# Fifteen input tiles made ahead, weight sums on another engine, a projection on six banks, an affine step in place, and a new order of products in one kernel

## The chip, the cores and the metric

One core of a Trainium2 chip runs the whole program as one launch. The time is device time in microseconds of that core, the median of three runs. Its engines are TensorE (PE, with PEld for loading weights into it), VectorE (DVE), ScalarE (ACT), GpSimd (POOL) and SyncE (SP), which issues nearly all DMAs. SBUF holds the tiles that the engines work on, and the eight PSUM banks hold what PE accumulates.

## What is computed

One decoder layer for a prompt of 2048 tokens and eight samples of 8 tokens each, 2112 token columns in all, model width 1024, everything in float32:

```python
mod = silu(c) @ w_ada + b_ada                      # six modulation vectors: sh1, sc1, g1, sh2, sc2, g2
h = rmsnorm(x, norm_mix_w) * (1 + sc1) + sh1
qkv, z, b, a, sq, sk, sv = split(h @ w_in)         # input projection
o_dn = deltanet(causal_conv4(qkv), z, b, a)        # gated DeltaNet, 4 heads, chunks
o_swa = attend(sq, sk, sv)                         # window of 128, 8 heads, sinks, relative bias
x = x + g1 * (concat(o_dn, o_swa) @ w_out)
h = rmsnorm(x, norm_ffn_w) * (1 + sc2) + sh2
gate, up = split(causal_conv3(h @ ffn_w_up) + ffn_conv_b)
x = x + g2 * ((silu(gate) * up) @ ffn_w_down)      # width 2816 in between
y = rmsnorm(x, final_norm_w)
```

The outputs are y for all tokens, the last inputs of both convolutions, the DeltaNet states and the window's keys and values.

## The kernel before

**Tiling.** Activations lie transposed, 128 channels on the partitions and tokens in columns. The tokens come in two halves: half 0 has two blocks of 512 columns, half 1 blocks of 384, 384 and 320 columns, the last with the samples' 64 (`HALVES`, line 37). A weight tile is 128 x 1024 (`load_split`, L325). Each float32 operand is split into a high part, a rounded copy made by ACT (L330), and a low part, the difference, made by DVE or POOL (L331); a product is then three matmuls, hi x hi, hi x lo and lo x hi (`gemm_steps`, L339).

**Order.** Work is written as generators that are interleaved: `beside(steps, filler, share)` runs a filler's steps between those of other work, `lockstep` takes one step of each of several in turn, `chain` one after the other. Every engine executes its own instructions in one fixed order, which a planner of the framework lays out when the program is built. An engine that waits therefore holds up all that stands behind it. A pool's tile with a tag and a number of buffers is a ring: a new tile of that tag waits until the oldest one has been read for the last time.

**Stages** (times from the trace, in us): until about 66 the modulation vectors and the first products of the input projection; to 237 `inproj(0, ...)` for rows 2 to 11, beside `tasks` (the rest of the modulation, `weight_sums` for units 0 to 5, the gates, and `x_rstd` for half 1); to 350 `inproj(0, ...)` for rows 12 to 21, beside `ahead(0)`, the DeltaNet's first two chunks; to about 730 `mixers(0)` (DeltaNet scan and attention) beside `inproj(1, ...)`, whose rest runs to 797; then `between(0)` with the output projection, `ffn_in` (residual, norm, h of the second branch) and the FFN's up projection; then the same for half 1; from 1657 to 2177 the second part of the up projection; from 2177 on `down_phase`.

**What the change touches.**

- `affine_h` (L235) makes h from x: a DMA loads x into a tile `ht` of the tag "cv" (L261 to L263), DVE multiplies it by scale and norm (L264), then either ACT adds the shift into `hi` (L270) and DVE makes `lo` (L271), or, for every second k, ACT adds the shift in place (L266), ACT casts (L267) and POOL makes `lo`. Where the source is a list of tiles already in SBUF (the first block of the kernel, and the last block of `ffn_in`), `ht` is still taken from "cv" and the list's tile is read. The samples' part (`hst`, L251) uses a "cv" tile as well.
- The ring "cv" has five buffers (`CV = 5`). It also holds `ev`, the output of a projection's convolution (`conv_block`: `rb`, a raw copy, at L537, `ev` or `cv` at L540 or L542, three taps on DVE at L547) and the other results of `in_evac` (L600 to L608).
- `second` makes all of half 1's h, 24 tiles and the samples' one, when half 0's projection gives up its last two h tiles, one block after the other.
- `inproj(1, ...)` accumulates in the two PSUM banks "acc"; `FREE_TAGS` names six banks, which `between` uses for its own projections.
- `weight_sums` (L1621) combines two rows of the down projection's weights in four DVE instructions of 128 x 512 (L1632 to L1635), through one buffer "suv", and stores them to `ws_d`; six of 11 units run beside the first input projection, the others later.
- `down_phase` (L1648) multiplies in seven products of half-size blocks instead of eight (a Strassen scheme), over two passes of tokens; each product has 11 k tiles and takes four output blocks by 11 x 3 matmuls. `DOWN` (L1643) gives the products' order, their weight operand (A or S), their token operand (B or T), and the outputs to which each adds. `get_t` loads the token operand and combines it where needed: T2 = B22 - T1, T4 = T1 + E. T1, T3 and E come from `ts_d`, which the up projection stores. All raw loads go to rings of `RAWS = 4`; "tr" and "wr" lie in the pool `ds`, "tx" and "x" in the pool `dr`, opened when the up projection's pools are closed. `norm` is the last RMSNorm with its stores, run as steps between later products.

Of the kernel before, what the change touches and what calls it, by code (L numbers as in the profile page):

```python
# [94 lines left out]
def kernel(  # L95
# [138 lines left out]

    def affine_h(hb, bi, hf, branch, rB, src, ks=range(KT), pool_too=lambda k: k % 2, smp=None):  # L235
# [21 lines left out]
        for k in ks:  # L257
            h, l = hi[:, k, :np_], lo[:, k, :np_]
            t = x = gw.tile([P, 512], F32, tag="cv", name="ht", bufs=CV)[:, :np_]
            if isinstance(src, list):  # L260
                x = src[k][:, :np_]  # L261
            else:
                nc.sync.dma_start(x, src[k, :, c0:c0 + np_])  # L263
# [354 lines left out]

    def inproj(hf, h, ic, ms, **kw):
        return project(ms, "in_ps", lambda m: load_split(I["w_inT"][m], nc.gpsimd if hf and m % 2 else nc.vector), h, hf,  # L620
                       lambda m, bi, ps: in_evac(hf, bi, m, ps, ic), **kw)
# [999 lines left out]
    def weight_sums(units, pool):  # L1621

        tt = nc.vector.tensor_tensor
        cut = lambda t: (t[:, :D // 2], t[:, D // 2:])
        for i in units:
# [17 lines left out]
    DOWN = [("A11", "B11", 1, True, [(0, 1)]), ("S2", "T2", 1, False, [(0, 2)]), ("S3", "T3", 2, False, [(1, 1), (1, 2)]),  # L1643
            ("S1", "T1", 2, True, [(1, 2)]), ("S4", "B22", 2, False, [(0, 2)]), ("A22", "T4", 1, True, [(1, 1)]),
            ("A12", "B21", 1, True, [(0, 1)])]
    NM = KT // 2

    def down_phase(ds, dr, pd):  # L1648
# [28 lines left out]
        def load(tag, src, n, most, bufs):  # L1677

            raw = (dr if tag == "tx" else ds).tile([P, most], F32, tag=tag, name=tag, bufs=bufs)[:, :n]
# [10 lines left out]
        w, t = {}, {}  # L1690
# [7 lines left out]
        def get_t(q, i, r):  # L1698
# [4 lines left out]
            get = lambda tag, name, r, bufs: load(tag, t_src(q, name, i, r), r.stop - r.start, big, bufs)  # L1703
            if name == "T2":
                raw, more = get("tr", "T1", r, RAWS), get("tx", "B22", slice(r.start, min(r.stop, PW)), RAWS)
                c = more.shape[1]
                nc.vector.tensor_tensor(raw[:, :c], more, raw[:, :c], ALU.subtract)
                if c < raw.shape[1]:
                    nc.scalar.mul(raw[:, c:], raw[:, c:], -1.0)
            elif name == "T4":  # L1710
                raw, more = get("tr", "T1", r, RAWS), get("tx", "E", r, RAWS)
                nc.vector.tensor_tensor(raw, raw, more, ALU.add)
            else:
                raw = get("tr", name, r, RAWS)
            t[q, i, r.start] = halves(ds, "t", raw, big, DR)

        def blocks_of(q, g=None):

            if q < ND or q % ND in (3, 4):
# [456 lines left out]
```

## Time and profile before

| | |
|---|---|
| runs shown | 2650.94 us median of 3 (2646.79 to 2656.68) |
| the profiled execution | 2652.56 us, of which the span of its instructions is 2650.8 us |
| mean granted TensorE clock | 0.990 |
| DMA | 445.31 MB in 325327 packets, mean 168 GB/s |

The profile shows one execution. Its span runs from the first to the last instruction; the execution's own time lies 1.8 us above it. The page gives the busy time of each engine, the chain of work that ended last, the costliest groups of instructions, and, with the trace, who made an engine wait, the single instructions in time, and for any stretch the busy time of each engine with the granted clock. TensorE's matmuls on 512 columns start 227 ns apart where nothing disturbs them, those on 384 columns 174 ns apart. In rows of one instruction the columns are start in us, duration in us, engine, line, operation, out <- in with shapes, and in brackets the idle time of the engine before it with what ended it; rows of a group have the count, then minimum, median and maximum in ns and the stretch in which they ran; rows of waits have the total, the count and the longest, in us.

### The profile page before, as it was taken

The numbers are of one execution on the slowest core, as the hardware profiler recorded it, in microseconds if no ns is written. First come the engines' busy times: TensorE is split into PE (matmuls) and PEld (weight loads), VectorE is DVE, ScalarE is ACT, GpSimd is POOL, SyncE is SP. The second block draws the span as 40 slices with busy tenths as digits, with TensorE's granted clock in tenths as the row PEclk, the third lists the DMA queues.
The fourth block names the chain that finished last, engine by engine and source line by source line (L and its number), as shares of the span: only waits on it lengthen the run. The fifth ranks groups of instructions, "written<-read, shape, count | busy, mean of one in ns | idle before, by whom it ended". The sixth has DMA issues, their size and how long they took to land.

```text
span 2650.8 us, 45631 instructions
## 1 busy us (share of the span) xinstructions
PE 2564.9 (97%) x16424; PEld 2223.7 (84%) x16424; DVE 1838.0 (69%) x3657; ACT 1284.4 (48%) x3124; POOL 757.6 (29%) x677
## 2 busy tenths in 40 slices
PE   7999989999999899999999999999999999999998
PEld 5677878888897787777777789999999997889988
DVE  7475469887443677888868664886777666676676
ACT  5453355564342455455444353554555554554343
POOL 2031133233332412223211123335555520020012
PEclk9999989999999999999999999999999999999999
DMA  7787454334456253343226357424555459678673
GB/s 288 247 301 236 134 151 118 101 97 115 106 176 205 103 144 98 105 108 102 76 92 215 130 181 225 144 67 156 171 170 186 166 183 302 214 237 279 214 250 130
DMA packets 325327, 445.31 MB, mean 168 GB/s; under 512 B 83267, under 2 KB 207268, under 8 KB 324836
## 3 DMA queue, kind: packets, MB, share of 16 engines
q1 hardware_dynamic: 325100, 442.39, 52.7%
q8 instruction: 129, 2.11, 0.3%
q14 instruction: 98, 0.80, 0.1%
HBM read 322.74 MB, written 120.57 MB: 167 GB/s over the span
## 4 chain that ended last, share of the span: by engine, by line
PE 70%; DVE 12%; DMA 9%; ACT 3%; issue 3%; SPq 2%; POOL 1%; DVEq 0%; POOLq 0%; ACTq 0%
PE up_ps L339 15%; PE dn_ps L1795 15%; PE in_ps L339 12%; PE uq_b L1585 5%; PE op_ps L339 4%; PE uq_c L1585 2%; PE uq_u L1585 2%; PE uq_g L1585 2%; DVE ev L547 2%; PE pv_ps L1007 1%; PE uq_a L1585 1%; DMA mt<-mixd 1%; PE as_ps L970 1%; DVE w_lo L331 1%; DMA suv<-in_w_downT_dram 1%
## 5 line engine op out<-in xcount | busy, mean ns | idle before, releaser
L339 PE MATMUL in_ps<-hi,w_hi 128*128 128x512 f32 (+2 forms) x880 | 320.4, 367 | 10.0 <-ACT ev L608 5.6
L339 PE MATMUL up_ps<-hi,w_hi 128*128 128x512 f32 (+2 forms) x808 | 315.0, 390 | 7.3 <-ACT cv L542 7.3
L339 PE MATMUL in_ps<-lo,w_hi 128*128 128x512 f32 (+2 forms) x880 | 316.6, 360 | 2.4 <-DVE lo L271 2.0
L339 PE MATMUL in_ps<-hi,w_lo 128*128 128x512 f32 (+2 forms) x880 | 314.9, 358 | 0.0
L339 PE MATMUL up_ps<-lo,w_hi 128*128 128x512 f32 (+2 forms) x808 | 313.9, 388 | 0.0
L339 PE MATMUL up_ps<-hi,w_lo 128*128 128x512 f32 (+2 forms) x808 | 311.8, 387 | 0.0
L1795 PE MATMUL dn_ps<-th,wh 128*128 128x512 f32 (+2 forms) x796 | 272.2, 343 | 4.5 <-DVE x L1263 4.2
L1795 PE MATMUL dn_ps<-tl,wh 128*128 128x512 f32 (+2 forms) x796 | 272.2, 342 | 3.6 <-DVE tl L1687 3.6
L1795 PE MATMUL dn_ps<-th,wl 128*128 128x512 f32 (+2 forms) x796 | 270.8, 342 | 0.0
L331 DVE TENSOR_TENSOR w_lo<-w_raw,w_hi 128x1024 fp32r<-128x1024 f32 x115 | 145.7, 1267 | 82.8 <-ACT w_hi L330 81.3
L330 ACT CAST w_hi<-w_raw 128x1024 fp32r<-128x1024 f32 x126 | 132.0, 1047 | 145.9 <-PE op_ps L339 52.2
L339 PEld LDWEIGHTS in_ps<-hi,w_hi 128*128 128x128 f32 x880 | 166.6, 190 | 36.7 <-issue 7.8
L339 PEld LDWEIGHTS in_ps<-lo,w_hi 128*128 128x128 f32 x880 | 167.1, 190 | 26.2 <-issue 7.6
L339 PEld LDWEIGHTS up_ps<-hi,w_hi 128*128 128x128 f32 x808 | 152.6, 189 | 41.9 <-issue 8.6
L339 PEld LDWEIGHTS up_ps<-lo,w_hi 128*128 128x128 f32 x808 | 152.7, 189 | 35.1 <-issue 10.7
L339 PEld LDWEIGHTS in_ps<-hi,w_lo 128*128 128x128 f32 x880 | 166.8, 190 | 15.6 <-issue 1.6
L339 PEld LDWEIGHTS up_ps<-hi,w_lo 128*128 128x128 f32 x808 | 152.4, 189 | 31.4 <-issue 5.3
L1795 PEld LDWEIGHTS dn_ps<-th,wh 128*128 128x128 f32 x796 | 150.7, 190 | 21.9 <-DVE x L1263 3.9
L1795 PEld LDWEIGHTS dn_ps<-tl,wh 128*128 128x128 f32 x796 | 150.9, 190 | 19.1 <-DVE tl L1687 3.9
L1795 PEld LDWEIGHTS dn_ps<-th,wl 128*128 128x128 f32 x796 | 150.8, 189 | 15.6
L1686 ACT CAST wh<-wr 128x512 fp32r<-128x512 f32 x149 | 92.1, 618 | 143.7 <-PE dn_ps L1795 115.5
L547 DVE SCALAR_TENSOR_TENSOR ev<-rb,cw,ev 128x512 f32<-128x512 f32 (+2 forms) x180 | 132.3, 739 | 31.4 <-ACT ev L540 29.6
(547 smaller groups left out, 6493.5 us busy)
## 6 DMA issues: line engine op xcount, KB each, us to landing
w_raw<-in_w_upT_dram SPq DMA_DIRECT2D x50, 512.0 KB
wada<-in_w_ada_dram SPq DMA_DIRECT2D x48, 512.0 KB
w_raw<-in_w_inT_dram SPq DMA_DIRECT2D x44, 512.0 KB
wr<-ws_d SPq DMA_DIRECT2D x88, 256.0 KB
w_raw<-in_w_outT_dram SPq DMA_DIRECT2D x34, 512.0 KB
d<-act_d SPq DMA_DIRECT2D x33, 512.0 KB
wr<-in_w_downT_dram SPq DMA_DIRECT2D x66, 256.0 KB
tr<-T_d SPq DMA_DIRECT2D x66, 256.0 KB
```

The source lines that it names most:

```text
L330: nc.scalar.copy(hi, raw)
L331: (eng or nc.vector).tensor_tensor(lo, raw, hi.bitcast(F32), ALU.subtract)
L339: nc.tensor.matmul(ps[:, :n], a[:, k, :], b[:, k, :n], start=first is not False and k == ks[0] and i == 0, stop=last is not False and k == ...
L547: nc.vector.scalar_tensor_tensor(out, src(j), w[:, j:j + 1], out, ALU.mult, ALU.add)
L970: nc.tensor.matmul(banks[v][:, 256 * g:256 * g + 256 - P * k0], qs[:, 2 * (g0 + g) + v], t[:, v, :2 - k0].rearrange("p w j -> p (w j)"), s ...
L1007: nc.tensor.matmul(pv_ps[64 * v:64 * v + 64, :], (vprev[0], vt)[half][:, 64 * v:64 * v + 64], PT[v, half], start=half == k0, stop=half == 1)
L1585: nc.tensor.matmul(bk[t][:, :nb], u[:, k], v[:, k], start=new and k == 0 and y == 0, stop=k == KG - 1 and y == 2, skip_group_check=True)
L1686: nc.scalar.copy(h, raw)
L1795: nc.tensor.matmul(acc[m, s][:, :n], w[q, i][a][:, c], th[b][:, v], start=new and i == 0 and y == 0, stop=i == KH - 1 and y == 2, skip_gro ...
```

## The change

It has five parts.

**A.** The first six units of `weight_sums` run on POOL (`nc.gpsimd`) instead of DVE; the later five stay on DVE.

**B.** A new generator `early_h` makes 15 of half 1's 24 h tiles (block 0, k 0 to 7, and block 1, k 0 to 6) in lockstep with `ahead(0)`: it loads x, lets DVE multiply and ACT add the shift, all in place, in buffers that belong to the mixers' pool and are not yet in use there (tags "xz", "qs", "kh", "kl", "u", "o", "nl", "pt" and "PT"). `affine_h` then finds such a tile in `made` and only copies it to `hi` (ACT) and makes `lo`.

**C.** `inproj` takes its PSUM tags from a list `in_tags`, ["acc"] at first; after `mixers(0)` it is set to `FREE_TAGS`, six banks in turn, for what is left of `inproj(1, ...)`.

**D.** Where `affine_h`'s source is a list, the affine is made in place in the list's tile, without a "cv" tile.

**E.** `down_phase` begins with the products of T1 and B22, whose operands stay in SBUF (`held`: 11 tiles each for T1 and B22, one buffer per tile); T2 and T4 are then made from the held tiles with no second load. "tr" moves to the pool `dr`; "wr" and T1's first four tiles lie in `ds`. The tiles x have one buffer instead of two. `FINAL` names, for each output, the product that completes it, and the norms start accordingly.

```diff
+    made = {}
+    def early_h(pool):
+        def spare(tag, bufs=1, size=1):
+            t = pool.tile([P, 4 * size, P], F32, tag=tag, name="he", bufs=bufs).rearrange("p h i -> p (h i)")
+            return [t[:, 512 * i:512 * i + 512] for i in range(size)]
+        room = iter(spare("xz") + spare("qs", 1, 2) + spare("kh") + spare("kl") + spare("u") + spare("o")
+                    + spare("nl", 3) + spare("nl", 3) + spare("nl", 3) + spare("pt") + [spare("PT", 4)[0] for _ in range(4)])
+        for i, t in enumerate(room):
+            bi, k = divmod(i, KT)
+            c0, n = HALVES[1][bi]
+            t = made[bi, k] = t[:, :n]
+            nc.sync.dma_start(t, I["xT"][k, :, c0:c0 + n])
+            nc.vector.scalar_tensor_tensor(t, t, MOD[:, 1, k, 0:1], rB_tile(1, bi), ALU.mult, ALU.mult)
+            nc.scalar.activation(t, t, AF.Identity, bias=MOD[:, 0, k, 0:1], scale=1.0)
+            yield True
...
-            t = x = gw.tile([P, 512], F32, tag="cv", name="ht", bufs=CV)[:, :np_]
+            if (bi, k) in made:
+                t = made.pop((bi, k))
+                nc.scalar.copy(h, t)
+                (nc.gpsimd if pool_too(k) else nc.vector).tensor_tensor(l, t, h.bitcast(F32), ALU.subtract)
+                yield True
+                continue
             if isinstance(src, list):
-                x = src[k][:, :np_]
+                t = x = src[k][:, :np_]
             else:
+                t = x = gw.tile([P, 512], F32, tag="cv", name="ht", bufs=CV)[:, :np_]
...
+    in_tags = ["acc"]
     def inproj(hf, h, ic, ms, **kw):
         return project(ms, "in_ps", lambda m: load_split(I["w_inT"][m], nc.gpsimd if hf and m % 2 else nc.vector), h, hf,
-                       lambda m, bi, ps: in_evac(hf, bi, m, ps, ic), **kw)
+                       lambda m, bi, ps: in_evac(hf, bi, m, ps, ic), **{"tags": in_tags, **kw})
...
-    def weight_sums(units, pool):
-        tt = nc.vector.tensor_tensor
+    def weight_sums(units, pool, eng):
+        tt = eng.tensor_tensor
...
-    DOWN = [("A11", "B11", 1, True, [(0, 1)]), ("S2", "T2", 1, False, [(0, 2)]), ("S3", "T3", 2, False, [(1, 1), (1, 2)]),
-            ("S1", "T1", 2, True, [(1, 2)]), ("S4", "B22", 2, False, [(0, 2)]), ("A22", "T4", 1, True, [(1, 1)]),
-            ("A12", "B21", 1, True, [(0, 1)])]
+    DOWN = [("S1", "T1", 2, True, [(1, 2)]), ("S4", "B22", 2, False, [(0, 2)]),
+            ("A11", "B11", 1, True, [(0, 1)]), ("S2", "T2", 1, False, [(0, 2)]), ("S3", "T3", 2, False, [(1, 1), (1, 2)]),
+            ("A22", "T4", 1, True, [(1, 1)]), ("A12", "B21", 1, True, [(0, 1)])]
+    FINAL = {(0, 2): 3, (1, 2): 4, (1, 1): 5, (0, 1): 6}
...
-            raw = (dr if tag == "tx" else ds).tile([P, most], F32, tag=tag, name=tag, bufs=bufs)[:, :n]
+            raw = (ds if tag in IN_DS else dr).tile([P, most], F32, tag=tag, name=tag, bufs=bufs)[:, :n]
...
+        w, t, held = {}, {}, {}
+        IN_DS = ["wr"] + [f"cT1_{i}" for i in range(RAWS)]
...
-            get = lambda tag, name, r, bufs: load(tag, t_src(q, name, i, r), r.stop - r.start, big, bufs)
-            if name == "T2":
-                raw, more = get("tr", "T1", r, RAWS), get("tx", "B22", slice(r.start, min(r.stop, PW)), RAWS)
-                c = more.shape[1]
-                nc.vector.tensor_tensor(raw[:, :c], more, raw[:, :c], ALU.subtract)
-                if c < raw.shape[1]:
-                    nc.scalar.mul(raw[:, c:], raw[:, c:], -1.0)
-            elif name == "T4":
-                raw, more = get("tr", "T1", r, RAWS), get("tx", "E", r, RAWS)
-                nc.vector.tensor_tensor(raw, raw, more, ALU.add)
+            n = r.stop - r.start
+            if name in ("T1", "B22"):
+                m = wide(q, 1) if name == "T1" else PW
+                held[name, i] = load(f"c{name}_{i}", t_src(q, name, i, slice(0, m)), m, big if name == "T1" else PW, 1)
+                raw = held[name, i][:, r]
+            elif name == "T2":
+                raw = dr.tile([P, big], F32, tag="tr", name="tr", bufs=RAWS)[:, :n]
+                nc.vector.tensor_tensor(raw[:, :PW], held["B22", i], held["T1", i][:, :PW], ALU.subtract)
+                if n > PW:
+                    nc.scalar.mul(raw[:, PW:], held["T1", i][:, PW:], -1.0)
             else:
-                raw = get("tr", name, r, RAWS)
+                raw = load("tr", t_src(q, "E" if name == "T4" else name, i, r), n, big, RAWS)
+                if name == "T4":
+                    nc.vector.tensor_tensor(raw, raw, held["T1", i][:, r], ALU.add)
             t[q, i, r.start] = halves(ds, "t", raw, big, DR)
...
-            if q < ND or q % ND in (3, 4):
+            if q < ND or q % ND in (0, 1):
...
-                    if j < 3:
+                    if j < FINAL[og, tg]:
...
-                x[o] = dr.tile([P, NM, big], F32, tag=f"x{o[0]}{o[1]}", name=f"x{o[0]}{o[1]}", bufs=2)
+                x[o] = dr.tile([P, NM, big], F32, tag=f"x{o[0]}{o[1]}", name=f"x{o[0]}{o[1]}", bufs=1)
...
-                finish = norm(*late, free[-2:], wait=2 - ip)
-            elif j == 6:
-                late = (1, 0, PW, x, sums[1], cols[1])
-            elif j == 2 and ip:
-                finish = norm(*late, free[-2:], wait=2)
+                rest(finish or ())
+                finish = norm(*late, free[-2:])
+            elif j == 6 and not ip:
+                finish = chain(finish, norm(1, 0, PW, x, sums[1], cols[1], free[-2:], wait=2))
...
-                  spaced(weight_sums(range(6), sa), 2)),
+                  spaced(weight_sums(range(6), sa, nc.gpsimd), 2)),
...
-            beside(ahead(0, mp), filler, SHARE[0])
+            beside(lockstep(ahead(0, mp), early_h(mp)), filler, SHARE[0])
...
+        in_tags[:] = FREE_TAGS
...
-            beside(lockstep(sample_delta(sp), sample_attend(sp), weight_sums(range(6, KH), sp)), filler, SHARE[2])
+            beside(lockstep(sample_delta(sp), sample_attend(sp), weight_sums(range(6, KH), sp, nc.vector)), filler, SHARE[2])
```

More of the change, by code (lines that the diff above doesn't have):

```diff
@@ L1688, in halves @@
             return h, l
-        w, t = {}, {}
+        w, t, held = {}, {}, {}
+        IN_DS = ["wr"] + [f"cT1_{i}" for i in range(RAWS)]
         def get_w(q, i):
```

## The prediction

> **What bounds the kernel now.** I read the page's span and busy times first, then who made TensorE wait, then the granted clock in short stretches.
>
> ```profile
> span 2650.8 us, 45631 instructions
> ...
> PE 2564.9 (97%) x16424; PEld 2223.7 (84%) x16424; DVE 1838.0 (69%) x3657; ACT 1284.4 (48%) x3124; POOL 757.6 (29%) x677
> ```
>
> PE is busy for 97% of the span. The change removes no matmul, so it can only win back time in which PE stands still or runs slowly. Who made it wait:
>
> ```profile
> PE up_ps L339 <- ACT cv L542: 7.3, 1, 7.3
> PE z_ps L785 <- DVE T L806: 7.2, 2, 6.4
> PE in_ps L339 <- ACT ev L608: 5.6, 2, 3.6
> ...
> PE op_ps L339 <- ACT ev L608: 2.4, 1, 2.4
> ```
>
> A few single waits stand out, all between stages. I took a stretch around each, and the stretches of low clock that go with them (columns: window, length, busy PE, PEld, DVE, ACT, POOL, granted clock, DMA share, GB/s):
>
> ```profile
> 230.00:244.00 14.00, 10.78 (x39) 8.42 (x38) 8.72 (x15) 2.64 (x5) 5.89 (x9) 0.76 0.70 228
> 350.00:392.00 42.00, 30.36 (x272) 27.17 (x271) 35.71 (x84) 30.09 (x92) 19.69 (x16) 0.80 0.53 143
> 786.00:804.00 18.00, 13.56 (x71) 11.69 (x70) 7.30 (x8) 8.35 (x15) 6.49 (x5) 0.91 0.62 187
> 908.00:926.00 18.00, 10.66 (x43) 8.40 (x42) 14.98 (x18) 10.16 (x18) 9.16 (x9) 0.81 0.04 15
> 2186.00:2216.00 30.00, 24.75 (x100) 19.41 (x99) 17.59 (x28) 11.95 (x22) 0.00 (x0) 0.94 0.90 313
> ...
> 235.90:243.00 7.10, 5.99 (x14) 4.74 (x15) 3.74 (x8) 1.77 (x3) 5.68 (x9) 0.52 0.74 240
> 355.40:362.30 6.90, 5.38 (x18) 5.38 (x18) 4.58 (x11) 5.68 (x18) 3.64 (x2) 0.51 0.62 197
> 375.90:386.10 10.20, 6.00 (x52) 4.51 (x52) 9.89 (x26) 5.17 (x13) 2.88 (x4) 0.51 0.21 57
> ...
> 799.20:802.70 3.50, 3.27 (x7) 2.24 (x8) 2.81 (x3) 1.85 (x4) 0.25 (x1) 0.51 0.38 117
> 915.20:922.10 6.90, 3.70 (x9) 2.93 (x10) 5.99 (x7) 4.05 (x8) 5.49 (x7) 0.51 0.00 0
> 2205.40:2208.90 3.50, 3.50 (x10) 2.69 (x10) 2.37 (x4) 0.62 (x1) 0.00 (x0) 0.52 1.06 397
> ```
>
> Length less PE busy is idle; of the time busy at half clock, half is lost. So the five places cost: **A** (230) 3.2 + 3.0 = 6.2 us; **B** (350) 11.6 + 2.7 + 3.0 = 17.3; **C** (786) 4.4 + 1.6 = 6.0; **D** (908) 7.3 + 1.9 = 9.2; **E** (2186) 5.3 + 1.8 = 7.1. The sum, 45.8 us or 1.7%, is about all that these edits can reach. Each meets one of them.
>
> **A: weight sums on POOL.** 24 adds and subtracts (six units of four) leave DVE's queue.
>
> ```profile
> 228.97 0.69 DVE L1632 TENSOR_TENSOR suv<-suv 128x512 f32<-128x512 f32 x1 [1.90 <-DMA suv<-in_w_downT_dram]
> ...
> 232.77 2.32 DVE L547 SCALAR_TENSOR_TENSOR ev<-rb,cw,ev 128x512 f32<-128x512 f32 x3
> 236.27 0.69 DVE L603 SCALAR_TENSOR_TENSOR ev<-ev,in_ps 128x512 f32<-128x512 f32 x1 [1.18 <-ACT ev L602]
> ...
> L1275 POOL TENSOR_TENSOR dsum<-dsum,sq 128x512 f32<-128x512 f32 x14 | 19.4, 1386 | 190.5 <-ACT sq L1274 190.5
> ```
>
> The convolution taps (L547) stand behind a unit: 1.9 us of waiting for its load and 4 x 0.69 = 2.8 us of work. ACT's silu and L603 (236.27) wait for the taps, and PE, idle for 3.2 us of this window, for L603. Without the unit the taps move up by nearly 4.7 us, more than the 3.2 us stall. POOL, busy for 5.9 of the window's 14 us, pays 4 x 1.39 = 5.6 us a unit (the 128x512 add of L1275), 2.8 us more; the units follow one another through one buffer, so the last ends up to 14 us later. Queued behind it on POOL are the first chunk's masks, which are not needed while input projections fill PE. If that cover fails, I allow 3 us of loss. **Value 5, between -3 and 6.2.**
>
> Against it speaks that POOL and DVE slow one another:
>
> ```profile
> L1632 DVE TENSOR_TENSOR suv<-suv x11: 677/692/1502, 139.4 to 1474.2; 128x512 f32<-128x512 f32 x11
> ...
> L284 POOL TENSOR_TENSOR xacc<-xacc,xst x21: 863/1210/1609, 128.6 to 188.7; 128x384 f32<-128x384 f32 x14, 128x320 f32<-128x320 f32 x7
> ```
>
> The DVE add takes 0.69 us, and up to 1.50 us in the stretch in which POOL adds. If each of POOL's four adds holds the taps up by the difference, 0.81 us, that gives back 3.2 us of the 4.7. What remains, 1.5 us, is less than the stall; A is then worth about 1.5, a rival below. [...]
>
> **B: fifteen tiles made early.** Where the projection changes to the second token half, 24 tiles of h (and the samples' one) are made at once:
>
> ```profile
> L264 DVE SCALAR_TENSOR_TENSOR ht<-ht,MOD,sg x24: 462/608/1346, 343.9 to 391.6; 128x384 f32<-128x384 f32 x16, 128x256 f32<-128x256 f32 x8
> ...
> L266 ACT ACTIVATE ht<-ht,MOD x12: 508/613/625, 346.8 to 392.3; 128x384 f32<-128x384 f32 x8, 128x256 f32<-128x256 f32 x4
> L267 ACT CAST hi<-ht x12: 392/502/523, 348.2 to 393.2; 128x384 fp32r<-128x384 f32 x8, 128x256 fp32r<-128x256 f32 x4
> ...
> 365.86 0.47 ACT L537 COPY rb<-in_ps 128x384 f32<-128x384 f32 x1
> ...
> 386.64 0.58 ACT L540 ACTIVATE ev<-in_ps,cw 128x384 f32<-128x384 f32 x1
> ...
> 376.03 1.67 DVE L251 TENSOR_TENSOR hst<-hst,MOD 128x512 f32<-128x512 f32 x1 [2.90 <-DMA hst<-in_xT_dram]
> ...
> 265.00:331.00 66.00, 66.00 (x420) 52.97 (x419) 31.50 (x99) 21.59 (x46) 7.85 (x11) 1.00 0.45 133
> ```
>
> Of one and the same product, ACT copies rb at 365.86 and writes ev only at 386.64: ev needs one of five "cv" buffers, and 25 tiles stand ahead in them. Fifteen leave this ring. At this place DVE is spared 15 x 0.608 = 9.1 us and ACT 15 x 0.613 - 8 x 0.502 = 5.2 us (seven of the 15 pay the affine and a cast now, eight the affine alone; made early, each pays one copy here, at the cast's price), besides 15 loads. The same work, with 15 loads more on SP, is put beside the stretch 265 to 331, where DVE is busy 31.5 of 66 us and PE all of it; there it costs nothing. If a load is late there, DVE waits, but PE has two accumulators of 5.4 us each as cover. What is left are ten tiles on five buffers, the wait for hst among them, so I don't take the whole 17.3. The early tiles sit in the attention's buffers; its loads wait until they are copied out. The first two thirds of the stall (3.6 us, and the 20 us of ev) should go, a wait for the last token block stay. **Value 11, between 3 and 17** (below nothing only by the rival S).
>
> **C: six accumulators.** Both waits at 786 are for a free accumulator. But the output projection needs its weights:
>
> ```profile
> 797.48 0.62 ACT L1182 CAST mixh<-mt 128x512 fp32r<-128x512 f32 x1 [2.23 <-DMA mt<-mixd]
> 798.01 1.04 ACT L330 CAST w_hi<-w_raw 128x1024 fp32r<-128x1024 f32 x1
> ```
>
> w_hi is there at 799.05 and PE goes on at 799.4. If ACT keeps its order, PE only waits longer once instead of twice, and 0.4 us is won; if the cast comes ahead of the late mixh, all 6.0. **Value 2.5.**
>
> **D: affine in place.** The same ring of five, in the next change of stage:
>
> ```profile
> 904.60 0.59 ACT L537 COPY rb<-up_ps 128x512 f32<-128x512 f32 x1 [1.89 <-PE up_ps L339]
> ...
> 917.59 0.76 ACT L542 ACTIVATE cv<-up_ps,fcb,fcw 128x512 f32<-128x512 f32 x1
> ...
> 908.76 3.38 DVE L264 SCALAR_TENSOR_TENSOR ht<-x,MOD,rb_ps 128x512 f32<-128x512 f32 x5 [4.49 <-PE rb_ps L222]
> ```
>
> The write of cv waits 13 us for a buffer, with eight tiles of h ahead. In place they take none, and cv is written at about 905.3, while DVE is idle (4.49 us). Then PE waits for h itself: eight tiles from 908.8 on, at 1.5 DVE operations of 0.74 us each, so up to 917.6, used by PE as they come; it ends about 4 us earlier than now, and part of the low clock goes. **Value 5, between 1 and 9.** At the start of the kernel the same edit is taken at nothing; the steps there are paced by the adaLN loads.
>
> **E: the down projection.** T1 and B22 are kept, 11 tiles each, which saves 33 loads a pass, 66 in all. After the start that is worth nothing: PE is busy throughout there.
>
> ```profile
> 2253.00:2319.00 66.00, 66.00 (x293) 54.68 (x292) 40.09 (x62) 32.92 (x60) 4.19 (x3) 1.00 0.66 213
> ...
> 2201.93 0.69 DVE L1707 TENSOR_TENSOR tr<-tx,tr 128x512 f32<-128x512 f32 x1 [7.88 <-DMA wr<-ws_d]
> ...
> 2189.30 0.32 SPq L1496 DMA_DIRECT2D E_d<-d  x1
> 2189.71 0.41 SPq L1827 DMA_DIRECT2D x<-x2T  x1
> 2190.18 2.26 SPq L1680 DMA_DIRECT2D tx<-act_d  x3
> ```
>
> At the start, DVE waits for the loads of L1707 with the tile that PE needs behind it; the new order has no such combination there. But only four T1 tiles lie in the pool "ds"; the rest lie in "dr", and the first loads into dr (x, tx) were issued only behind the last store of the up projection, at 2189.3. PE enters this stage at 2177 and has 4 x 12 matmuls x 0.225 (66.00 us for 293 in the window above) = 10.8 us of work with four tiles, up to 2187.8. Issued at 2189.7, landed in 3 us and split in 1.3, the fifth comes at about 2194: 6.2 us idle with some half clock, about today's loss. If dr is free at 2177, all 7.1 goes. If the load takes as long as the first tx (2190.2 to 2201.9), PE idles 15 + 1.8 and E loses 10. **Value 1, between -10 and 7.** The norms and the single x buffers lie beside products of 30 us each: nothing.
>
> **The sum.** 5 + 11 + 2.5 + 5 + 1 = 24.5 us off the execution's 2652.6 (span 2650.8): **2628 us**. The median shown, 2650.9, is 0.06% below that execution; I let the two stand for one.
>
> **Rivals.**
> - The late ten tiles keep the ring full: B gives 3, in all 16.5: 2636. For it, hst's load alone stopped DVE for 2.9 us.
> - POOL holds DVE up: A gives 1.5: 2632.
> - T1 is late by the full landing time: E is -10, in all 13.5: 2639. The issue at 2189.7 speaks for it, the short list of loads ahead against it.
> - All five stalls vanish: 2607. Against it stand C's weights and D's h.
> - **S, slower:** the attention's qs, kh, kl and nl buffers, held by early tiles, come free only about 356 to 360, and PE's fixed order keeps the attention's scores ahead of the products, as at 351.7 now. PE idles some 10 us more, with 3.4 us of half clock, beside today's stall; no B, with A, C, D and E at their weak ends (-3, 0.4, 1, -3): 2652.6 + 13.4 + 4.6 = 2671. It decides from the point where the first qs cast comes after about 360.
>
> **How the numbers follow.** Forecast 0.45, ring 0.17, POOL 0.08, late T1 0.13, all gone 0.08, S 0.09. The range 2608 to 2650 leaves out S and part of "all gone". 0.5%, 13 us, is about what a measurement of this kernel can tell from no change: below 2639 lie the forecast, the POOL case, "all gone", most of "ring" and half of "late T1": 0.70. Within: 0.21. Slower: 0.09.
>
> **What would show it.** A right: no wait of in_ps for L603 near 237, POOL's adds between 139 and 250. B: L540 within 3 us of its L537, no wait of z_ps. C: L330 before 797. D: L542 right after its L537. E: the first T1 load into dr before or behind the last E_d store. Wrong would be a PE busy time that grows, or new waits of over 3 us in the stretches from 398 to 729.

## The result and the profile after

The changed kernel takes 2629.04 us (median of 6 runs, 2625.73 to 2633.16), the kernel before beside it 2648.74 us (6 runs, 2646.79 to 2656.68). The ratio is 0.9921, with a 95% interval of 0.9904 to 0.9938. The medians differ by 19.7 us; the profiled execution took 2631.26 us, 21.3 us less than that of the kernel before. From L264 on, line numbers of the changed kernel lie 26 to 32 above those of the kernel before (L339 is L365, L540 is L566, L603 is L629, L1795 is L1827).

The page's span and busy times:

```profile
span 2629.5 us, 45388 instructions
...
PE 2559.6 (97%) x16424; PEld 2220.9 (84%) x16424; DVE 1841.3 (70%) x3633; ACT 1288.8 (49%) x3140; POOL 797.7 (30%) x708
```

TensorE executes the same 16424 matmuls; its busy time falls by 5.3 us (less low clock: the mean granted clock is 0.993, before 0.990), and the rest of the 21.3 us is idle time that is gone. POOL has 40 us more work, most of it part A's. Who made TensorE wait now (engine, tile, releaser: total, times, longest, in us; the tiles ending in _ps are accumulators: in_ps of the input projection, op_ps of the output projection, up_ps of the FFN's up projection, dn_ps of the down projection, rb_ps of the norm's factor, u_ps of the DeltaNet):

```profile
PE dn_ps L1827 <- ACT th L1715: 5.1, 1, 5.1
PE op_ps L365 <- DVE w_lo L357: 4.5, 6, 1.3
PE rb_ps L222 <- DVE dg L218: 4.3, 4, 1.7
PE u_ps L813 <- DVE Y L861: 3.7, 2, 3.3
PE op_ps L365 <- ACT w_hi L356: 3.0, 1, 3.0
PE up_ps L365 <- DVE lo L297: 1.9, 1, 1.9
...
PE in_ps L365 <- DVE ev L629: 1.8, 1, 1.8
...
PE up_ps L365 <- ACT sg L568: 1.5, 1, 1.5
```

The waits of 7.3, 6.4, 3.6 and 3.2 us are gone. A wait of 5.1 us (down projection), one of 3.3 us (Y, in the DeltaNet of half 0) and one of 3.0 us (output projection) have come. The stretches, with the columns of the prediction's windows (length, busy PE, PEld, DVE, ACT, POOL, granted clock, DMA share, GB/s):

```profile
188.00:202.00 14.00, 11.41 (x39) 8.64 (x39) 10.58 (x11) 5.48 (x13) 9.34 (x7) 0.76 0.54 200
...
350.00:392.00 42.00, 39.08 (x342) 34.01 (x342) 36.48 (x87) 28.02 (x94) 19.92 (x16) 1.00 0.40 116
606.00:624.00 18.00, 14.74 (x82) 14.03 (x81) 13.77 (x44) 3.32 (x8) 3.56 (x4) 0.81 0.39 117
...
780.00:792.00 12.00, 8.26 (x38) 6.75 (x37) 4.20 (x4) 5.11 (x9) 3.83 (x3) 0.86 0.64 186
...
896.00:908.00 12.00, 8.60 (x33) 6.46 (x32) 11.40 (x15) 8.42 (x15) 4.91 (x4) 0.86 0.06 23
...
2165.00:2182.00 17.00, 11.87 (x42) 9.05 (x41) 10.06 (x14) 5.14 (x12) 0.00 (x0) 0.80 0.69 251
```

Of these, only the stretch from 350 to 392 (part B's) now runs at full clock with little idle time. For gains by place I counted each matmul by its median interval to the next one of its shape in the kernel before, and compared the times at which both traces reach the same sum ("the count" below):

| stretch of the kernel before, us | place | gained, us |
|---|---|---|
| 0 to 76 | start | -2.1 |
| 76 to 305 | A | -0.3 |
| 305 to 405 | B | 13.7 |
| 405 to 623 | mixers of half 0 | 6.1 |
| 623 to 666 | the wait for Y | -6.3 |
| 666 to 875 | C's place (all of it at 788 to 835) | 0.8 |
| 875 to 925 | D | 3.8 |
| 925 to 2168 | | 1.6 |
| 2168 to 2256 | E, start | 0.3 |
| 2256 to end | E, rest | 3.4 |

### The profile page after: what moved, and what is told of

It reads as the page before. It is cut to its first block, busy times and chain, and to the rows that moved or that the text cites. A ratio compares the mean times of both kernels' runs of the same rounds, so it can differ in the third digit from the quotient of the medians.

```text
span 2629.5 us, 45388 instructions
## 1 busy us (share of the span) xinstructions
PE 2559.6 (97%) x16424; PEld 2220.9 (84%) x16424; DVE 1841.3 (70%) x3633; ACT 1288.8 (49%) x3140; POOL 797.7 (30%) x708
## 4 chain that ended last, share of the span: by engine, by line
PE 77%; DVE 9%; DMA 6%; ACT 2%; issue 2%; POOL 2%; SPq 1%; POOLq 0%; DVEq 0%; ACTq 0%
PE up_ps L365 18%; PE dn_ps L1827 16%; PE in_ps L365 13%; PE op_ps L365 5%; PE uq_b L1613 5%; PE uq_c L1613 2%; PE uq_u L1613 2%; PE uq_g L1613 2%; PE uq_a L1613 1%; PE pv_ps L1035 1%; PE as_ps L998 1%; DVE ev L573 1%; DMA mt<-mixd 1%; PE u_ps L813 1%; PE z_ps L813 1%
## 5 line engine op out<-in xcount | busy, mean ns | idle before, releaser
L365 PE MATMUL in_ps<-hi,w_hi 128*128 128x512 f32 (+2 forms) x880 | 319.5, 366 | 3.5 <-DVE ev L629 1.8
L365 PE MATMUL in_ps<-lo,w_hi 128*128 128x512 f32 (+2 forms) x880 | 316.4, 360 | 1.3 <-DVE lo L297 1.0
L365 PE MATMUL in_ps<-hi,w_lo 128*128 128x512 f32 (+2 forms) x880 | 316.2, 360 | 0.0
L365 PE MATMUL up_ps<-hi,w_hi 128*128 128x512 f32 (+2 forms) x808 | 314.3, 389 | 1.5 <-ACT sg L568 1.5
L365 PE MATMUL up_ps<-lo,w_hi 128*128 128x512 f32 (+2 forms) x808 | 313.4, 388 | 1.9 <-DVE lo L297 1.9
L365 PE MATMUL up_ps<-hi,w_lo 128*128 128x512 f32 (+2 forms) x808 | 311.7, 387 | 0.0
L1827 PE MATMUL dn_ps<-th,wh 128*128 128x512 f32 (+2 forms) x796 | 271.4, 343 | 5.1 <-ACT th L1715 5.1
L1827 PE MATMUL dn_ps<-tl,wh 128*128 128x512 f32 (+2 forms) x796 | 272.4, 342 | 0.0
L1827 PE MATMUL dn_ps<-th,wl 128*128 128x512 f32 (+2 forms) x796 | 270.8, 342 | 0.0
L365 PEld LDWEIGHTS in_ps<-hi,w_hi 128*128 128x128 f32 x880 | 166.2, 190 | 29.9 <-issue 8.8
L365 PEld LDWEIGHTS in_ps<-lo,w_hi 128*128 128x128 f32 x880 | 167.2, 190 | 21.0 <-issue 3.8
L365 PEld LDWEIGHTS up_ps<-lo,w_hi 128*128 128x128 f32 x808 | 152.3, 188 | 37.3 <-issue 10.7
L365 PEld LDWEIGHTS up_ps<-hi,w_hi 128*128 128x128 f32 x808 | 152.3, 188 | 35.8 <-issue 8.6
L365 PEld LDWEIGHTS in_ps<-hi,w_lo 128*128 128x128 f32 x880 | 166.9, 190 | 18.1 <-issue 3.6
L365 PEld LDWEIGHTS up_ps<-hi,w_lo 128*128 128x128 f32 x808 | 152.1, 188 | 31.6 <-issue 5.3
L1827 PEld LDWEIGHTS dn_ps<-th,wh 128*128 128x128 f32 x796 | 150.7, 190 | 20.9 <-ACT th L1715 5.6
L573 DVE SCALAR_TENSOR_TENSOR ev<-rb,cw,ev 128x512 f32<-128x512 f32 (+2 forms) x180 | 140.1, 784 | 38.9 <-ACT ev L566 34.3
L1827 PEld LDWEIGHTS dn_ps<-tl,wh 128*128 128x128 f32 x796 | 151.0, 190 | 16.0 <-DVE tl L1716 0.4
L1827 PEld LDWEIGHTS dn_ps<-th,wl 128*128 128x128 f32 x796 | 151.0, 190 | 15.6
```

The lines of the kernel that those rows point to most:

```text
L365: nc.tensor.matmul(ps[:, :n], a[:, k, :], b[:, k, :n], start=first is not False and k == ks[0] and i == 0, stop=last is not False and k == ...
L573: nc.vector.scalar_tensor_tensor(out, src(j), w[:, j:j + 1], out, ALU.mult, ALU.add)
L1827: nc.tensor.matmul(acc[m, s][:, :n], w[q, i][a][:, c], th[b][:, v], start=new and i == 0 and y == 0, stop=i == KH - 1 and y == 2, skip_gro ...
```

## The experiments

Theory: each part acts at its own place, as in the table. Rival: every edit makes the planner lay out the program anew, and the waits that come or go elsewhere are of the same size. All runs, each beside runs of the kernel before:

| run | median us (lowest to highest) | ratio to before (95% interval) |
|---|---|---|
| changed kernel | 2629.04 (2625.73 to 2633.16) | 0.9921 (0.9904 to 0.9938) |
| e9_after_again | 2629.71 (2624.84 to 2632.92) | 0.9939 (0.9927 to 0.9951) |
| e1_without_A | 2633.41 (2628.75 to 2639.09) | 0.9943 (0.9930 to 0.9956) |
| e10_only_A | 2655.55 (2650.22 to 2660.31) | 1.0039 (1.0027 to 1.0051) |
| e7_sums_late | 2635.49 (2633.50 to 2638.26) | 0.9956 (0.9940 to 0.9973) |
| e2_without_B | 2645.94 (2640.30 to 2650.31) | 0.9994 (0.9984 to 1.0004) |
| e6_B_loads_only | 2630.58 (2623.39 to 2633.82) | 0.9934 (0.9911 to 0.9957) |
| e3_without_C | 2627.35 (2624.42 to 2628.39) | 0.9919 (0.9906 to 0.9932) |
| e4_without_D | 2631.21 (2628.45 to 2637.33) | 0.9938 (0.9921 to 0.9956) |
| e5_without_E | 2635.32 (2630.07 to 2638.96) | 0.9955 (0.9937 to 0.9973) |
| e8_six_T1 | 2637.68 (2636.10 to 2639.30) | 0.9964 (0.9952 to 0.9975) |
| e11_T1_by_pool | 2623.12 (2621.78 to 2626.74) | 0.9917 (0.9904 to 0.9929) |
| e12_together | 2621.34 (2614.79 to 2623.96) | 0.9899 (0.9882 to 0.9917) |

The unaltered kernel's two ratios, 0.9921 and 0.9939, lie 0.2% apart. So a difference of less than some 5 us between two rows is not resolved by the times, and for such sizes the waits in the traces decide.

### Part A

```diff
-                  spaced(weight_sums(range(6), sa, nc.gpsimd), 2)),
+                  spaced(weight_sums(range(6), sa, nc.vector), 2)),
```

> The changed kernel with part A undone: all weight sums on DVE again. Theory (A moved the stall): beside the first input projection the changed kernel's PE stands 1.7 us for rb_ps at 191.4, behind POOL's row of adds, runs 3.4 us at half clock, and stands 1.8 us at 258.4; without A these go and the wait of in_ps for L603's ev with some 3 us and its low clock comes back, so the time stays within 2 us of the changed kernel's 2629. Rival (A is worth the 5 us of the prediction, and the waits at 191 and 258 come from something else): they stay, the old stall is added, and the time is about 2634.

Without A, the wait for L629's ev is back (first fence, the waits of e1 from 180 to 270), and those for rb_ps are gone. In the changed kernel the step behind rb_ps looks like this (second fence, its timeline on POOL and DVE: start, duration, operation, idle time before):

```profile
PE in_ps L365 <- DVE ev L629: 5.5, 4, 3.5
```

```profile
178.50 9.14 POOL L310 TENSOR_TENSOR xacc<-xacc,xst 128x320 f32<-128x320 f32 x7
189.44 1.33 POOL L310 TENSOR_TENSOR xacc<-xacc,xst 128x320 f32<-128x320 f32 x1 [1.80 <-ACT rb L562]
190.74 0.86 POOL L144 TENSOR_TENSOR rtok<-rsq,mhalf 128x3 f32<-128x3 f32 x1
191.58 1.27 POOL L1660 TENSOR_TENSOR suv<-suv 128x512 f32<-128x512 f32 x1
...
191.63 3.35 DVE L218 TENSOR_SCALAR dg<-cst,rtok 128x128 f32<-128x128 f32 x3 [1.59 <-POOL rtok L144]
```

POOL works through a row of `x_rstd`'s own adds (L310) before it comes to rtok, the reciprocal root of the block before. DVE waits 1.6 us for rtok with the convolution taps behind it, its three dg then take 3.35 us beside POOL's suv (their median is 0.28 us each), and PE stands 1.7 us and runs 6.8 us at half clock (0.51 from 194.0 to 200.9). So the stall has moved from one queue to the other. The median without A, 2633.4, is 4 us higher, nearer to the rival's 2634 than to the theory's 2629, but not resolved; the profiled execution of e1, 2630.57 us, is no longer than that of the changed kernel.

Part A alone, on the kernel before (the first six units from DVE to POOL, as in the change):

> The kernel before with part A alone. Theory (A only moves the wait at its own place): the wait of in_ps for L603 near 237 is gone, waits for rb_ps near 190 or for ev near 258 stand in its place, and the time is within 3 us of the kernel before. Rival 1 (the prediction's term, A is worth 5 us): 3.5 us or more under the kernel before. Rival 2 (POOL and DVE hold each other up so that A loses): 2 us or more above it.

It is slower by 9.3 us, and resolved: rival 2's outcome, but its mechanism is not shown to be the cause. Its own place is clear of the old stall (230 to 244), the stall for rb_ps has come (188 to 202), and the place of B has become worse (windows of e10, then of the kernel before):

```profile
350.00:412.00 62.00, 46.55 (x348) 40.68 (x347) 56.54 (x127) 40.55 (x128) 31.29 (x24) 0.81 0.38 113
230.00:244.00 14.00, 14.00 (x64) 11.59 (x63) 6.33 (x7) 3.82 (x8) 6.40 (x5) 1.00 0.59 211
188.00:202.00 14.00, 11.29 (x48) 8.86 (x46) 10.53 (x12) 6.38 (x16) 9.35 (x7) 0.88 0.55 204
```

```profile
350.00:412.00 62.00, 50.12 (x400) 44.72 (x399) 55.23 (x131) 42.91 (x137) 29.91 (x23) 0.86 0.48 133
188.00:202.00 14.00, 14.00 (x69) 11.66 (x69) 9.49 (x16) 5.64 (x13) 2.02 (x2) 1.00 0.62 226
```

From 350 to 412, PE is busy 3.6 us less at a lower clock, though the last unit had ended on POOL by 245. What differs there is the plan. Which moved instruction does the harm was not traced. Nor do these two traces show the whole loss: the profiled execution of e10 took 2651.32 us, no more than that of the kernel before (2652.56), though the medians are 9.3 us apart. Where the 9.3 us arise stays open.

All eleven units late, on DVE beside the samples' attention:

```diff
-                  spaced(weight_sums(range(6), sa, nc.gpsimd), 2)),
-            beside(lockstep(sample_delta(sp), sample_attend(sp), weight_sums(range(6, KH), sp, nc.vector)), filler, SHARE[2])
+            beside(lockstep(sample_delta(sp), sample_attend(sp), weight_sums(range(KH), sp, nc.vector)), filler, SHARE[2])
```

> The changed kernel, but all eleven weight sum units run late, on DVE beside the samples' attention, and none beside the first input projection. Theory (any unit beside the first projection holds up either DVE's or POOL's queue there): neither the wait for ev at about 233 nor those at 191 and 258 show, and the time is 2621 to 2626. Rival (those waits have other causes, or the six units hold up DVE as much at the later place): within 2 us of 2629 or above.

A miss. Up to 307 this kernel is 6.9 us ahead of the changed one by the count above, but it loses 5.0 us between 393 and 477 and 9.4 us between 1497 and 1664, where op_ps waits for w_lo 6.7 us in place of 3.7. And one wait of 1.6 us for rb_ps at 177 is there without any unit:

```profile
PE rb_ps L222 <- DVE dg L218: 1.8, 2, 1.6
```

So `x_rstd`'s own adds on POOL can be enough for that wait, which is hardly longer (1.7 us) with the units on POOL. In e1, where POOL has the same adds and no unit there either, the wait does not come: it hangs on the plan, and the units' share in it stays open.

### Part B

```diff
-            beside(lockstep(ahead(0, mp), early_h(mp)), filler, SHARE[0])
+            beside(ahead(0, mp), filler, SHARE[0])
```

> The changed kernel with part B undone: no tiles made early, all 24 made where the projection changes half. Theory (B is most of the gain, by its own place): the waits at about 350 and 372 come back, PE falls back by 14 to 20 us between them, and the time is 2640 to 2649. Within that, if the wait of 3.3 us for Y near 611 is a price of B, it goes and the time is nearer to 2640; if it is chance, it stays and the time is nearer to 2649. Rival (C, D or the rest of the plan give most): under 2636.

The median rises by 16.9 us and all but reaches the kernel before. First fence, e2: one window, and ACT's rb and ev of the first product of half 1. Second fence, the same of the changed kernel:

```profile
350.00:412.00 62.00, 46.09 (x359) 40.73 (x359) 57.14 (x132) 39.64 (x127) 32.64 (x24) 0.81 0.42 119
...
367.34 0.46 ACT L563 COPY rb<-in_ps 128x384 f32<-128x384 f32 x1
...
391.70 0.57 ACT L566 ACTIVATE ev<-in_ps,cw 128x384 f32<-128x384 f32 x1
```

```profile
350.00:412.00 62.00, 59.08 (x482) 53.40 (x482) 54.48 (x140) 40.23 (x138) 23.45 (x21) 1.00 0.43 128
...
365.78 0.48 ACT L563 COPY rb<-in_ps 128x384 f32<-128x384 f32 x1
...
369.17 0.58 ACT L566 ACTIVATE ev<-in_ps,cw 128x384 f32<-128x384 f32 x1
```

With B, ev follows its rb after 3.4 us, without it after 24 us. PE is busy 13 us longer in the 62 us, at full clock. Not all of the 13 us is B's stall of the kernel before: that kernel was busy for 50.12 us of this window, and A alone had brought it down to 46.55 (both above), which is nearly e2's 46.09. Without B, A does harm here; with B it makes little difference (60.10 us in e1, 59.08 with A). So part of what e2 loses is A's harm, and the five parts cannot be added up one by one. The 3.3 us wait for Y is not in e2, nor in e1; it is in every other kernel that has B, with units on POOL or without (e7), at 2.5 to 3.3 us. So neither B (e1 has it) nor units on POOL (e7 has none) decide it: it belongs to the plan.

```diff
+                nc.vector.scalar_tensor_tensor(t, t, MOD[:, 1, k, 0:1], rB_tile(1, bi), ALU.mult, ALU.mult)
+                nc.scalar.activation(t, t, AF.Identity, bias=MOD[:, 0, k, 0:1], scale=1.0)
                 nc.scalar.copy(h, t)
```

(and the same two lines taken out of `early_h`)

> The changed kernel, but the fifteen early tiles are only loaded early; DVE's multiply and ACT's shift are done where the projection changes half. Theory (the ring of five buffers was the cause, as the prediction has it first): the early buffers alone lift it, ev follows its rb within some 5 us, and the time stays within 4 us of 2629. Rival (the 9 us of DVE and 5 us of ACT work at that place were the cause): most of the stalls of the kernel before come back and the time is 2638 to 2649.

The time is the changed kernel's, but the run does not tell the two theories apart: the planner put the multiply (L279) at 254 to 266 all the same, where it was (L251) in the changed kernel.

```profile
L279 DVE SCALAR_TENSOR_TENSOR he<-he,MOD,sg x15: 582/612/965, 254.4 to 266.1; 128x384 f32<-128x384 f32 x15
```

```profile
L251 DVE SCALAR_TENSOR_TENSOR he<-he,MOD,sg x15: 583/615/970, 252.9 to 264.5; 128x384 f32<-128x384 f32 x15
```

It shows that B does not need the multiply and the shift written at the early place: given the spare buffers, the plan makes the tiles early by itself. How much of the gain is the ring and how much the 14 us of DVE and ACT work moved away stays open.

### Parts C and D

```diff
-        in_tags[:] = FREE_TAGS
```

> The changed kernel with part C undone: the rest of the half 1 projection on two banks. Theory (the end of that projection is set by the output projection's weights, not by banks): two waits of about 2 us come back in place of the one of 3.0 us for w_hi, and the time stays within 1.5 us of 2629. Rival (C gives the 2.5 us of the prediction or more): 2631.5 to 2635.

The theory holds for the time: 2627.35, the same as with C. The two waits that come back are shorter than expected. The waits from 770 to 800, first of e3 with its window, then of the changed kernel (its window, 780 to 792, stands above):

```profile
PE in_ps L365 <- ACT ev L634: 1.3, 1, 1.3
PE op_ps L365 <- ACT ev L634: 0.4, 1, 0.4
PE op_ps L365 <- DVE w_lo L357: 0.4, 1, 0.4
...
778.00:790.00 12.00, 9.84 (x53) 8.10 (x52) 3.63 (x4) 5.21 (x10) 3.87 (x3) 1.00 0.63 194
```

```profile
PE op_ps L365 <- ACT w_hi L356: 3.0, 1, 3.0
PE op_ps L365 <- DVE w_lo L357: 0.8, 1, 0.8
```

C joins short waits into one of 3.0 us for the output projection's weights. After that the clock halves for 3.4 us (0.51 from 788.0 to 791.4, mean 0.86 in its window); after the short ones it does not (1.00). By the count, e3 gains 2.8 us on the changed kernel at this place: C as it stands loses there.

```diff
-            if isinstance(src, list):
-                t = x = src[k][:, :np_]
-            else:
-                t = x = gw.tile([P, 512], F32, tag="cv", name="ht", bufs=CV)[:, :np_]
+            t = x = gw.tile([P, 512], F32, tag="cv", name="ht", bufs=CV)[:, :np_]
+            if isinstance(src, list):
+                x = src[k][:, :np_]
+            else:
                 nc.sync.dma_start(x, src[k, :, c0:c0 + np_])
```

> The changed kernel with part D undone: the affine of a list's tiles goes through a tile of the ring of five. Theory (D gives the 3.8 us seen at its place in ffn_in): a wait of up_ps for cv of about 7 us comes back with its low clock, and the time is 2632 to 2634.5. Rival 1 (D also pays at the start of the kernel, where the same edit applies): over 2635. Rival 2 (the stall was lifted by the new plan, not by D): 2629.

The wait is back (first fence, the waits of e4 from 880 to 920), while in the changed kernel cv is written right behind its rb (second fence, ACT's timeline). By the count, e4 loses 4.4 us at this place; the times alone (2 us) do not resolve it, and the median, 2631.2, lies just below the range expected.

```profile
PE up_ps L365 <- ACT cv L568: 7.3, 1, 7.3
```

```profile
892.58 0.59 ACT L563 COPY rb<-up_ps 128x512 f32<-128x512 f32 x1 [1.89 <-PE up_ps L365]
893.07 0.79 ACT L568 ACTIVATE cv<-up_ps,fcb,fcw 128x512 f32<-128x512 f32 x1
```

### Part E

The edit of e5 puts the old `down_phase` with its `DOWN` back.

> The changed kernel with part E undone: the down projection as before. Theory (E exchanges one stall at its start for another of the same size and gains about 3 us at its end, where x had to be read while accumulators were awaited): PE's wait of 5.1 us at the stage's start becomes one of about 3.6 us with a second of 1.4, the waits of 0.9 and 1.7 us near the end come back, and the time is 2631 to 2634. Rival (the 66 loads saved are worth something in the middle of the stage too): over 2635.

E's waits of e5 (2160 to 2560) against one of 5.1 us with E:

```profile
PE dn_ps L1823 <- DVE x L1291: 5.2, 3, 2.6
PE dn_ps L1823 <- DVE tl L1715: 4.5, 2, 4.3
```

They are the waits expected, somewhat longer at the start (4.3 and 2.6 us; 0.9 and 1.7 near the end). In the middle of the stage the count shows no difference, so the rival falls, though the time, 2635.3, is at its bound; E is worth 3.7 us (against the kernel before) to 7 us (against e5) by the count.

```diff
-        IN_DS = ["wr"] + [f"cT1_{i}" for i in range(RAWS)]
+        IN_DS = ["wr"] + [f"cT1_{i}" for i in range(6)]
```

> The changed kernel, but six of T1's eleven tiles lie in the pool that is free before the up projection ends, not four. Theory (the stall at the start of the down projection is the fifth tile, whose load waits for the last store of E_d): the 5.1 us wait and its low clock go or shrink below 1.5 us, and the time is 2621 to 2626. Rival (the larger pool reaches into memory that is in use longer, so that all its early loads are late, or the loads themselves are late at that place): 2629 or more.

The rival is right: slower by 8 us. With two more tiles in the pool `ds`, all its loads, the first weights too, come behind the last store of E_d (SP's queue, then the wait), as they would if the larger pool reached into memory still in use:

```profile
2164.39 0.32 SPq L1524 DMA_DIRECT2D E_d<-d  x1
2164.76 0.45 SPq L1709 DMA_DIRECT2D wr<-ws_d  x1
...
PE dn_ps L1827 <- ACT th L1715: 13.7, 1, 13.7
```

So six tiles do not fit early; five were not tried. The other way is to leave the memory and change the queue:

```diff
+            if via:
+                nc.gpsimd.dma_start(raw, src)
+            else:
                 fetched[:] = [nc.sync.dma_start(raw, src).ins]
...
+                                     q == 0 and name == "T1" and RAWS <= i < 2 * RAWS)
```

> The changed kernel, but T1's tiles 4 to 7 of the first product are loaded by POOL's queue, not SP's. Theory (the fifth tile's memory is free once PE has read the up projection's h at about 2159, and its load at 2171.5 was late only because SP's queue stood before it, at the last stores of the up projection): the load is issued before 2165, the 5.1 us wait shrinks to about 1.2 us, since ACT casts the tile only after its last work for the up projection at 2170, most of the low clock goes, and the time is 4 to 6 us under that of the unaltered changed kernel. Rival (the memory itself is in use until 2171, or a load from POOL's queue takes much longer): the wait stays at 4 us or more and the time is the same or longer.

First fence, SP's queue in the changed kernel; second, POOL's and SP's queue in e11 and the waits:

```profile
2171.10 0.32 SPq L1524 DMA_DIRECT2D E_d<-d  x1
2171.51 0.41 SPq L1709 DMA_DIRECT2D cT<-T_d  x1
```

```profile
2156.67 2.41 POOL L1710 DMA_DIRECT2D cT<-T_d  x4 [0.30 <-issue]
...
2166.72 0.32 SPq L1524 DMA_DIRECT2D E_d<-d  x1
...
PE dn_ps L1831 <- ACT th L1718: 2.8, 2, 1.7
```

The theory is right. The load is issued 10 us ahead of the last E_d store, no longer 0.4 us behind it; the wait falls from 5.1 us to 1.1 us with a second of 1.7, and the time is 6.6 us under that of e9, the unaltered kernel measured beside the same runs of the kernel before (0.9917 against 0.9939; the intervals overlap by 0.0002). By the count, 4.2 us of this lie at the start of the down projection against the first profile of the changed kernel, and 3.4 us against e9's. The rest lies elsewhere and is not shown to be the edit's.

The unaltered kernel again:

> The changed kernel once more, unaltered, for the spread of its single waits between executions. Theory (the wait of 3.3 us for Y near 611 hangs on how long the round trip of AM through memory takes, 7.5 us in the one profile and 5.5 in that of the kernel before, and on whether POOL then works; the lengths of the low clock come in steps of 3.4 us): the same waits appear at the same instructions, but that one and the low clock after each differ by up to 3.4 us and more, and the profiled time differs by several us from 2631. Rival (the waits belong to the plan alone): all waits within 0.3 us of those of the first profile.

The rival is right for the wait for Y, 3.06 us where it was 3.26; it is no chance of a round trip. Other waits moved more: 2.6 us for L629's ev where it was 1.8, 2.5 for w_hi where it was 3.0. What differs most is the low clock: after the wait at 191 it lasted 6.8 us in one execution (0.76 in the window above) and did not come in the other:

```profile
188.00:202.00 14.00, 11.63 (x56) 9.24 (x55) 11.37 (x12) 6.04 (x16) 9.55 (x7) 1.00 0.57 205
```

Last, e11's edit with part C undone and x's first load later (`if i in ((1, 5) if q else (5, 7)):`):

> The changed kernel with three edits together: T1's tiles 4 to 7 by POOL's queue, the first x tile of the down projection loaded four k steps later, and part C undone. Theory (each acts at its own place): the two short waits near 780 in place of one of 2.5 to 3.0 us run with no low clock after them, worth about 2.8 us; the wait of 1.7 us near 2176 for the weights, which come in behind x's 1 MB, shrinks below 0.5 us; with the 6 us of the tiles by POOL the time is 2617 to 2621. Rival (undoing C is worth nothing, as its own interval allows, and the DMA engines are full there whatever comes first): 2622 to 2625, with the second wait still over 1 us.

It has the lowest median, 2621.34 us, between what theory and rival expected. Undoing C gains 2.6 us at its place by the count against e11. The waits at the start of the down projection stay at 2.6 us together, 1.5 and 1.1, so moving x did not do what was expected. Against e11 the time is not resolved (0.9899 against 0.9917); against the changed kernel e12 is 7.7 us faster; its interval lies below that of e9 and overlaps that of the first comparison.

## Why the prediction held, point by point

The forecast was 2628 us and 24.5 us of gain; measured were 2629.04 us and, between the profiled executions, 21.3 us. The sum is right partly because errors cancel: by the count, A, C and D gave 8.2 us less than their terms, B and E 5.2 us more.

- **What bounds the kernel**: right. Most of the gain lies at the places quoted; the exceptions are E's end, 3.4 us, and what the new plan shifts between them. One sign that was named for being wrong did come: a new wait of over 3 us between 398 and 729, the one for Y.
- **A, 5 us**: wrong. At its place A brings -0.3 us. The step that failed is the list of what else POOL has to do there: the masks were named, `x_rstd`'s rtok was not, on which DVE and PE wait (how much of that wait is the units' stays open, as e7 shows). The rival "POOL holds DVE up" foresaw the direction, with 1.5 us. The signs named for A all came (no wait for L603's ev near 237, POOL's adds from 141 to 243), and still it gained nothing. A alone costs 9.3 us, which no step foresaw; in the changed kernel the medians leave room for up to 4 us of gain, but no trace places it.
- **B, 11 us**: right mechanism, undersized at its place. The changeover gained 13.7 us and the stage after it 6.1, near the 17.3 of which I took two thirds, because the ten late tiles did not stop the ring again (3.4 us from rb to ev). If the new wait for Y is charged to B, it takes 6.3 us back, and 13.5 is left. e2 loses 16.9 us, with A's harm at this place in it. Of the signs, rb to ev came at 3.4 us where under 3 was named, and of the 7.2 us for which z_ps waited for T, 1.2 remain. S, the slower rival, did not occur: the early tiles were copied out between 338 and 353, and the scores began at 357.
- **C, 2.5 us**: too high, and probably of the wrong sign. The place gained 0.8 us, but without C it is better still, by 2.8 us in e3 and 2.6 in e12, so the 0.8 us come from the other parts. The reason stated holds: the weights set the end, and their cast (785.4) still follows the late mixh (784.9). The step that failed is "PE only waits longer once instead of twice, and 0.4 us is won": the one wait of 3.0 us is longer than e3's 1.3 and 0.4 together, and 3.4 us at half clock follow it (0.51 from 788.0 to 791.4), none the short ones (1.00 in e3), which was not foreseen. The medians (2627.35 without C) do not resolve this.
- **D, 5 us**: right, 3.8 us. As worked out, PE next waits for h itself, 1.9 us for its low part (L297), with 3.4 us of low clock (0.50 from 904.0 to 907.4); another 1.5 us before that is for an accumulator that ACT writes out late (sg, L568), between its steps for h.
- **E, 1 us**: the start was right, step by step: the fifth tile was issued 0.4 us behind the last E_d store, as predicted, its cast began 3.6 us after the issue (3 forecast for the landing), and idle time and low clock cost as much as before (5.1 us of waiting, 6.2 forecast, and 4.9 us of work at a clock of 0.50). "The norms and the single x buffers: nothing" was too low by 3 us; the two waits for accumulators near 2563 are gone, and without E they come back.

## What to carry to other kernels

Where one engine's instructions run in a fixed order, moving work to an idle engine can move it in front of whatever short step that engine does for the others (here rtok, 0.86 us on POOL, for which DVE waited 1.6 us); list those steps first, the single small ones above all. When a pool is needed at a change of stage, look at buffers that the next stage has not begun to use: that was worth most here (13.7 us at its place). A load that is late may wait for its place in a queue and not for its memory: T1's fifth tile was issued at 2171.5 from SP's queue and at 2156.7 from POOL's, which gained about 4 us at that place without any change of buffers. And undo each part in the finished kernel before you credit it with what its place gained: C's place gained, and is better still without C; A did harm at B's place, and hardly any once B was there.

## What the runs showed of the hardware

After a wait the low clock lasted 3.4 us (in the changed kernel from 788.0 to 791.4 and from 904.0 to 907.4, granted clock 0.51 and 0.50), twice that (194.0 to 200.9, 613.9 to 620.7 and 2173.8 to 2180.6, 0.50 to 0.51) and once, in the kernel before, 10.2 us (375.9 to 386.1, 0.51). It differs between executions of one kernel: at 191, after a wait of 1.7 us with two of 0.3 and 0.6 us behind it, it lasted 6.8 us in the first and did not come in e9 (0.76 and 1.00 from 188 to 202). It also differs between kernels: from 776 to 800, where the changed kernel waits for w_hi, PE is idle for 3.7 us there and 3.5 us in e1, and the granted clock is 0.93 (3.4 us low) and 0.86 (6.7 us low, an estimate from that mean). In e3, after waits of 1.3 and 0.4 us, it is 1.00 over the same stretch.

Beside POOL's instructions some of DVE's took longer; what held them up was not traced. A DVE operation of 32x15 took 2.27 us beside POOL's w_lo and ended 0.04 us after it (median of its 17 in each of the two kernels: 0.17 us); and eight subtractions of 128x384, beside POOL's seven of the same kind, took 1.25 us in the median, 0.55 us at best:

```profile
609.89 2.27 DVE L761 TENSOR_SCALAR TU<-G 32x15 f32<-32x15 f32 x1 [2.40 <-DMA G<-at_d]
...
609.76 2.36 POOL L357 TENSOR_TENSOR w_lo<-w_raw,w_hi 128x1024 fp32r<-128x1024 f32 x1 [3.35 <-ACT w_hi L356]
...
L282 DVE TENSOR_TENSOR lo<-he,hi x8: 550/1250/1369, 339.0 to 353.6; 128x384 fp32r<-128x384 f32 x8
L282 POOL TENSOR_TENSOR lo<-he,hi x7: 1165/1332/1457, 339.2 to 353.0; 128x384 fp32r<-128x384 f32 x7
```
